# Two transformer layers on one core: output transposes as a stage of their own, modulation chunks in two steps, another order of the streams

## The chip, the cores and the metric

One core of a Trainium2 chip. The metric is the device time of one execution in microseconds, the median of the runs.

## What is computed

The block runs two trunk layers over 512 latent tokens and 256 context tokens of width 1024, in float32. Layer 0 is differential attention with 8 heads, layer 1 is neighbourhood attention with 16 heads of 64. Each is followed by a squared-ReLU MLP of width 4096, and each sub-layer is normed, shifted, scaled and gated by vectors that come from the conditioning (the modulation).

```python
def diff_attend(q, k, v, lam):
    s = jnp.einsum('bqhmd,bkhmd->bhmqk', q, k).astype(jnp.float32) * ATTN_SCALE
    p = jax.nn.softmax(s, axis=-1)
    w = (p[:, :, 0] - lam * p[:, :, 1]).astype(v.dtype)
    return jnp.einsum('bhqk,bkhe->bqhe', w, v)
...
mod_l = jnp.split((jax.nn.silu(c) @ w_mod[i] + b_mod[i])[:, None, :], N_MOD, axis=-1)
h_l = modulate(rms_norm(x, norm1_g[i]), mod_l[0], mod_l[1])
...
x = x + mod_l[2] * y_l
x = x + mod_l[5] * squared_relu_mlp(modulate(rms_norm(x, norm2_g[i]), mod_l[3], mod_l[4]), w_mlp1[i], w_mlp2[i])
```

In layer 0 the output of a head is normed per token (`subln_g`) before the output projection. The context tokens go through the same weights and read only context.

## The kernel before

All matmuls of the model run as three passes over operands that are split into a high and a low part (`PASSES`), so each weight tile is loaded raw (tile `R`, two buffers, queue of SP), copied by ACT (L116) and subtracted by POOL (L117) into a tile `W`. The raw modulation weights use the same two buffers (L130).

**The stages.** Setup with head 0's projections (to about 102 us of the profile), the heads of layer 0 (to 518), its output projection (to 645), its MLP (to 1230), the groups of layer 1, two heads each (to 1550), its output projection (to 1650), its MLP.

**A head of layer 0.** Two generators describe it. `qkv0` projects the 768 tokens in six tiles of 128 (24 matmuls of 384 columns each, in two halves, L370), norms queries and keys (`qk_normed`: ACT L377 and L379, DVE L381, a power on POOL L258, DVE L383), splits the values (L422, L423), rotates on POOL (L427 to L437), and after two tiles turns queries and keys with PE (`turn`, L445, bank `PC`) and splits them (`q_split`, `k_split`, L393 to L407). The fourth step of `k_split`, the copy of the low part into the other half of the partitions, is POOL's (L407). `attend0` works on six query tiles in stages: stage 0 is the scores (L492, one buffer `PS` of three banks, then maximum, exponential and the difference of the two maps on DVE and ACT, L497 to L504), stage 1 the transposes of the map (L516, bank `PB`, split by ACT L518 and DVE L519 into `X`), stage 2 the weighting with the values (L527, bank `PB`) and the norm of the output (ACT L530 and L534, DVE L531 and L252, power on POOL L258, DVE L536, into `O`). The output transpose `turn` (L480, bank `PB`, read out by ACT L481) of a tile is issued at the end of the weighting of the tile after it, and that of the last tile at the very end of the head; then the head's output goes to memory.

**A group of layer 1** has the same shape (`qkv1`, `attend1`): projections in L370, turns of queries and keys in L589 and L591, scores in L632, transposes in L662, weighting in L677 with its read-out in L682 and L683.

**What sets the order.** `run` steps the generators by a string: `q` the projections of the next head, `a` the attention of the present one, `b` the first stage of the next, `p` the rest of an earlier projection, `r` the projection after that, `l` the load of a modulation chunk, `m` its computation. Inside the head and group loops PE keeps the order of this program (`manual_schedule`); ACT, DVE and POOL are ordered by a scheduler at build time. Each engine works its own list strictly in order. `mod_chunk` computes 256 modulation values: 8 matmuls (L222) into a bank `PA`, a copy by ACT (L225), and right behind these on PE either two small matmuls (L235) or one (L227) that read the copy, and a step on DVE.

Of the kernel before, what the change touches and what calls it, by code (L numbers as in the profile page):

```python
# [10 lines left out]
F32 = mybir.dt.float32  # L11
# [7 lines left out]
P = 128  # L19
# [15 lines left out]

ORD_HEAD = "aa qq aa q p q l a q a q m l a qq a q aaa q m aaa qq a q b a q aa"
ORD_OUT0 = "q l aaaa p a m l a m a q a q aaa q aaa qq a q a qq aa Q"
ORD_FIRST1 = "qqqqqqqqqqqq rr q a"
ORD_GROUP = "qq a q a qq a a q a q a aa qqq a a r q a r b"
ORD_GROUP7 = "qq a q a qq a a q a q a aa l qqq a a m q a b"  # L40
ORD_OUT1 = "q a l a m a l aa m a q aa q a q a qq a l m Q"
# [15 lines left out]
class Block:  # L57
# [158 lines left out]
    def mod_chunk(self, l, n, raws):  # L216
# [7 lines left out]
        sb = self.sbt('T', [P, 256])  # L224
        nc.scalar.activation(sb, ps[:, 0:256], AF.Copy)  # L225
        if sec in (2, 5):
            nc.tensor.matmul(ps[0:32, 256:512], self.sel, sb, start=True, stop=True)  # L227
            br = self.sbt('T', [2, 256])
            nc.scalar.dma_start(
                br, self.a["bmod"][l, sec:sec + 1, 256 * qtr:256 * qtr + 256].to_broadcast([2, 256]))  # L230
            nc.vector.tensor_add(br, ps[0:2, 256:512], br)
            nc.scalar.dma_start(self.gates[l, sec // 3, :, 256 * qtr:256 * qtr + 256], br)
            return
        for b in range(2):
# [6 lines left out]
        if sec % 3 == 0:  # L241
            nc.vector.tensor_add(self.mB[:, l, norm, ks, :], src, bias)
        else:
            t = self.sbt('SQ', [P, 2, 2])
            nc.vector.tensor_add(t, src, bias)
            nc.vector.scalar_tensor_tensor(
                self.mA[:, l, norm, ks, :], t, 1.0, self.gT[:, norm, l, ks, None].to_broadcast([P, 2, 2]),
                op0=ALU.add, op1=ALU.mult)


# [148 lines left out]

    def k_split(self, ps, kh, kl, cols):  # L400
        nc = self.nc
        lo, hi = slice(0, 64), slice(64, 128)
        for m, (a, b) in enumerate(((lo, hi), (hi, lo))):
            nc.scalar.activation(kh[a, m, cols], ps[a], AF.Copy)
            nc.vector.tensor_sub(kl[a, m, cols], ps[a], kh[a, m, cols].bitcast(F32))
            nc.scalar.activation(kh[b, m, cols], ps[a], AF.Copy)
            nc.gpsimd.tensor_copy(kl[b, m, cols], kl[a, m, cols].bitcast(F32))  # L407

# [4 lines left out]
    def qkv0(self, w, hT, out, accs=None, tag='Q'):  # L413
# [25 lines left out]
        def turn(i):  # L439
# [7 lines left out]
            self.q_split(ps[:, 0:256], q, cols)  # L447
            self.k_split(ps[:, 256:512], kh, kl, cols)

# [19 lines left out]
    def attend0(self, h, qkv, last=None):  # L469
        nc = self.nc  # L470
        q, kh, kl, v = qkv
        oTs = []
        late = []

        def turn(i, on):
# [4 lines left out]
            nc.tensor.transpose(pt[:, :P], on, self.ident)  # L480
            nc.scalar.activation(oT[:, P * i:P * i + P], pt[:, :P], AF.Copy, scale=self.subg[:, 0:1])  # L481
# [39 lines left out]
        def weigh(i):  # L521
# [4 lines left out]
            for x, kt in jobs:  # L526
# [15 lines left out]
        soft, wTs = {}, {}  # L542
        scores(0)
        yield
        for stage, i in ATT0:
            (scores, turned, weigh)[stage](i)
            yield
        turn(*late.pop(0))
        if last is None:
            nc.scalar.dma_start(self.oT0[h], oTs[0])  # L550
        else:
            last.append(oTs[0])


# [14 lines left out]
    def qkv1(self, w, hT, out, tag='H'):  # L569
# [14 lines left out]
        def turn(i0):  # L584
# [7 lines left out]
            if i0:  # L592
                self.q_split(ps[:, 256:512], q, slice(P * i0 - 256, P * i0), gain=self.gqk)
            self.k_split(ps[:, :256], kh, kl, slice(P * i0, P * i0 + 256))
# [262 lines left out]
class Mods:  # L857


    def __init__(self, b, todo):  # L860
        self.b, self.todo, self.ready = b, todo, []

    def load(self, early=False):
        if self.todo:
            self.ready.append(self.b.mod_load(*self.todo.pop(0), early))

    def chunk(self):
        if self.ready:
            self.b.mod_chunk(*self.ready.pop(0))


def run(mods, order, **streams):


    for s in order.replace(" ", ""):
        if s == "l":
            mods.load()
        elif s == "m":
            mods.chunk()
        elif s.isupper():  # L880
# [6 lines left out]
def hybrid_block(tc, a, out):  # L887
    nc = tc.nc
    with ExitStack() as ctx, ExitStack() as st:
# [19 lines left out]
        with b.psum_phase("psA", **PS_ATTN0):  # L909
            att = b.attend0(0, cur)  # L910
            run(mods, "a", a=att)
            ahead = iter(())
            with tc.manual_schedule(engines={mybir.EngineType.PE}):
                for h in range(1, HEADS0):
# [9 lines left out]
            run(mods, ORD_OUT0, a=att, p=ahead, q=b.project(0, a["woa"], b.oT0, last, 0, lambda i: xs[i], 'H', 'Q', 'S', done))  # L924
            xh, hT2 = done
# [124 lines left out]
```

## Time and profile before

| | us |
|---|---|
| median of 3 runs | 2017.05 (2016.19 to 2019.93) |
| the profiled execution | 2019.41 |
| its span | 2017.6 |
| mean granted TensorE clock | 0.954 |
| PE busy | 1814.1 |
| DVE, ACT, POOL busy | 1156.3, 810.3, 808.7 |

A window row gives a stretch of the span and its length, then the busy time of each engine with the number of its instructions, then the clock granted to PE, the share of DMA and GB/s. A row of waits gives engine, line and tile of the waiting instruction, who ended the wait, the total, the number and the longest. A row of the timeline gives start and length, engine, line, operation, tile written and tiles read, how many instructions are merged, and in brackets how long the engine stood before it and who ended that.

### The profile page before, as it was taken

What the parts mean: (1) busy time and instruction counts of PE and PEld (TensorE: products, weight loads), DVE (VectorE), ACT (ScalarE), POOL (GpSimd) and SP (SyncE); (2) the same over time, 40 slices, a digit from 0 to 9 for tenths busy, and PEclk for the clock granted to TensorE, in tenths of its full rate; (3) what the DMA queues carried; (4) which work ended last, traced back from release to release, by engine and by line L of the source; (5) the groups of instructions that cost most, each with busy time, mean ns of one, the idle gap of its engine ahead of it and who ended that gap; (6) DMA issues with size and microseconds to landing.
All of it is one profiled execution on the core that took longest, in us unless ns stands there. A gap on an engine that the chain in (4) does not pass through costs nothing.

```text
span 2017.6 us, 27149 instructions
## 1 busy us (share of the span) xinstructions
PE 1814.1 (90%) x10256; PEld 1588.0 (79%) x10256; DVE 1156.3 (57%) x2159; ACT 810.3 (40%) x1819; POOL 808.7 (40%) x716
## 2 busy tenths in 40 slices
PE   6497887888789999999999998898888889999998
PEld 5386777788568988888889887888887678888886
DVE  4566666766666434343343586677767574444447
ACT  4355555655634221221222134656656333222331
POOL 3635554544522221222232345444453234443443
PEclk9698888999799999999999998999999889999999
DMA  7212212121612332332422233222233422323232
GB/s 289 68 38 81 66 61 81 53 71 56 212 63 84 104 114 96 126 126 96 129 79 64 63 87 92 53 53 53 60 82 106 136 89 84 104 95 95 86 102 73
DMA packets 59299, 185.03 MB, mean 92 GB/s; under 512 B 7392, under 2 KB 13856, under 8 KB 55584
## 3 DMA queue, kind: packets, MB, share of 16 engines
q1 hardware_dynamic: 53424, 173.44, 28.1%
q10 hardware_dynamic: 5744, 9.85, 1.4%
q8 instruction: 81, 1.33, 0.3%
q14 instruction: 50, 0.41, 0.1%
HBM read 174.45 MB, written 8.81 MB: 91 GB/s over the span
## 4 chain that ended last, share of the span: by engine, by line
PE 67%; DVE 11%; POOL 7%; issue 5%; ACT 5%; DMA 3%; SPq 0%; ACTq 0%; POOLq 0%; DVEq 0%
PE PD L794 21%; PE PA L370 11%; PE PA L829 11%; PE PB L829 9%; PE PA L723 3%; POOL W L117 2%; PE PA L222 2%; POOL SQ L258 1%; PE PS L492 1%; POOL X L566 1%; PE PB L677 1%; PE PB L527 1%; PE PQ L360 1%; ACT E L498 1%; DVE SA L497 1%
## 5 line engine op out<-in xcount | busy, mean ns | idle before, releaser
L117 POOL TENSOR_TENSOR W<-R,W 128x1024 fp32r<-128x1024 f32 (+1 forms) x200 | 449.5, 2255 | 643.5 <-ACT W L116 629.6
L116 ACT ACTIVATE W<-R 128x1024 fp32r<-128x1024 f32 (+1 forms) x204 | 200.5, 993 | 462.2 <-PE PB L829 375.1
L794 PE MATMUL PD<-Q,W 128*128 128x384 f32 (+1 forms) x1584 | 291.6, 334 | 1.2 <-DVE Q L295 0.7
L794 PEld LDWEIGHTS PD<-Q,W 128*128 128x128 f32 x1584 | 271.8, 188 | 13.9 <-issue 5.4
L370 PE MATMUL PA<-W,H 128*128 128x384 f32 x1008 | 204.9, 355 | 0.0
L803 DVE TENSOR_TENSOR N<-N 128x768 f32<-128x768 f32 (+1 forms) x64 | 64.4, 1008 | 223.5 <-ACT N L799 117.1
L794 PE MATMUL PD<-H,W 128*128 128x512 f32 (+1 forms) x816 | 184.2, 382 | 3.4 <-DVE H L296 2.5
L370 PEld LDWEIGHTS PA<-W,H 128*128 128x128 f32 x1008 | 185.1, 199 | 1.0
L258 POOL TENSOR_TENSOR SQ<-SQ,half 128x4 f32<-128x4 f32 (+1 forms) x96 | 97.1, 1012 | 212.2 <-DVE SQ L381 210.5
L370 PE MATMUL PA<-W,Q 128*128 128x384 f32 (+1 forms) x1008 | 177.4, 331 | 1.1 <-POOL W L117 1.1
L794 PEld LDWEIGHTS PD<-H,W 128*128 128x128 f32 x816 | 149.5, 192 | 32.9 <-DVE H L296 2.7
L829 PE MATMUL PA<-W,H 128*128 128x512 f32 x648 | 165.4, 395 | 2.5 <-DVE T L835 2.3
L370 PEld LDWEIGHTS PA<-W,Q 128*128 128x128 f32 x1008 | 163.8, 197 | 1.9 <-POOL W L117 1.9
L829 PEld LDWEIGHTS PA<-W,H 128*128 128x128 f32 x648 | 119.3, 188 | 30.0 <-issue 4.5
L829 PE MATMUL PB<-W,H 128*128 128x512 f32 x504 | 130.3, 391 | 0.0
L829 PE MATMUL PA<-W,Q 128*128 128x512 f32 x432 | 110.4, 395 | 2.2 <-ACT Q L805 1.6
L829 PEld LDWEIGHTS PB<-W,H 128*128 128x128 f32 x504 | 94.3, 188 | 18.5
L498 ACT ACTIVATE E<-PS,SA 128x768 f32<-128x768 f32 (+1 forms) x96 | 72.9, 760 | 72.4 <-DVE SA L497 72.2
L829 PEld LDWEIGHTS PA<-W,Q 128*128 128x128 f32 x432 | 81.2, 188 | 22.1 <-ACT Q L805 2.4
L840 DVE TENSOR_TENSOR H<-PA,H 128x512 f32<-128x512 f32 x78 | 53.7, 688 | 73.2 <-PE PA L829 73.2
L497 DVE TENSOR_REDUCE SA<-PS 128x1 f32<-128x768 f32 (+1 forms) x96 | 74.5, 776 | 32.8 <-ACT E L498 18.5
L492 PE MATMUL PS<-Q,Q 128*128 128x256 f32 (+1 forms) x320 | 71.5, 360 | 22.3 <-ACT E L498 12.0
(215 smaller groups left out, 3131.5 us busy)
## 6 DMA issues: line engine op xcount, KB each, us to landing
R<-in_w_dram SPq DMA_DIRECT2D x128, 512.0 KB
W<-in_wmod_dram SPq DMA_DIRECT2D x28, 1024.0 KB
R<-in_wmod_dram SPq DMA_DIRECT2D x40, 512.0 KB
R<-in_wqa_dram SPq DMA_DIRECT2D x32, 384.0 KB
R<-in_wqb_dram SPq DMA_DIRECT2D x32, 384.0 KB
X<-in_rpb_dram SPq DMA_DIRECT2D x48, 128.0 KB
R<-in_woa_dram SPq DMA_DIRECT2D x8, 512.0 KB
R<-in_wob_dram SPq DMA_DIRECT2D x8, 512.0 KB
```

The source lines that it names most:

```text
L116: nc.scalar.activation(w[:, 0, :n], raw, AF.Copy)
L117: (eng or nc.gpsimd).tensor_sub(w[:, 1, :n], raw, w[:, 0, :n].bitcast(F32))
L258: nc.gpsimd.tensor_tensor(r, ss, self.half[:, :n], op=ALU.pow)
L370: nc.tensor.matmul(acc[:, :n], hT[kt][:, x, P * i:P * i + P], w[kt // 2][:, y, o:o + n], start=(kt == 0 and p == 0), stop=(kt == KT - 1 an ...
L492: nc.tensor.matmul(s[:, c0:c1], q[:, m, P * i:P * i + P], k[:, m, c0:c1], start=p == 0, stop=p == 1)
L497: nc.vector.tensor_reduce(mx, s, op=ALU.max, axis=AX, negate=True)
L498: nc.scalar.activation(e[:, m, :nk], s, AF.Exp, bias=mx[:, 0:1], accum_out=sm[:, m:m + 1])
L723: nc.tensor.matmul(ps, oHL[h][:, x, c:c + P], w[h // 2][:, y, 512 * (h % 2):512 * (h % 2) + 512], start=(first and h == hs[0] and p == 0), ...
L794: nc.tensor.matmul(ps[:, at:at + b1 - b0], w[kt // 4][:, x, o:o + P], hT[kt][:, y, b0:b1], start=(kt == 0 and p == 0), stop=(kt == KT - 1 ...
L803: nc.vector.tensor_mul(r, r, r)
L829: nc.tensor.matmul(ps, hd[:, x, P * i - c0:P * i - c0 + P], w[f][:, y, 512 * n:512 * n + 512], start=(f == 0 and p == 0), stop=(f == len(h ...
L840: nc.vector.tensor_add(av, ps, av)
```

## The change

Six edits belong together.

1. The output transpose of layer 0 is a stage of its own, number 3, in the table `ATT0`, and stands two or more stages behind its weighting. The last weighting and the last two transposes of a head are run by the next head's iteration (stream `z`), ahead of the turn of that head's last queries and keys.
2. `mod_chunk` is a generator of two steps: `m` issues the matmuls and ACT's copy, `n` the small matmuls and the rest. One more chunk is computed in the output stage of layer 0 and one fewer in its MLP.
3. Head 1 has an order of its own (`ORD_HEAD0`), which begins with two tiles of its projections; before, head 0's first scores came first and outside the loop.
4. The streams of the heads and groups are interleaved in another order (one of the lines stands in the diff for all).
5. In layer 1 the turns of queries and keys come one or two half tiles later, and three steps of the next group's projections stand in a group in place of two.
6. In the last turn of queries and keys of a head or group, `k_split` makes the second low part by a DVE subtraction from PSUM in place of POOL's copy.

```diff
-ORD_HEAD = "aa qq aa q p q l a q a q m l a qq a q aaa q m aaa qq a q b a q aa"
+ORD_HEAD0 = "l qqqq a q a q a m aa q n a q aa q a l a q aa m aa q n aaa q a q aa b q a"
+ORD_HEAD = "a q z a q z aa q z p q l a q aa q m l q a q a n q aa m aa q n aa q aa qq aa b q a"
...
-ATT0 = ((0, 1), (1, 0), (2, 0), (1, 1), (2, 1), (0, 2), (0, 3), (1, 2), (2, 2), (0, 4), (1, 3), (2, 3),
-        (0, 5), (1, 4), (2, 4), (1, 5), (2, 5))
+ATT0 = ((0, 1), (1, 0), (2, 0), (1, 1), (2, 1), (0, 2), (3, 0), (0, 3), (1, 2), (3, 1), (2, 2), (0, 4), (1, 3),
+        (3, 2), (2, 3), (0, 5), (1, 4), (3, 3), (2, 4), (1, 5), (2, 5), (3, 4), (3, 5))
@@ mod_chunk
         nc.scalar.activation(sb, ps[:, 0:256], AF.Copy)
+        yield
         if sec in (2, 5):
@@ k_split
-            nc.gpsimd.tensor_copy(kl[b, m, cols], kl[a, m, cols].bitcast(F32))
+            if soon:
+                nc.vector.tensor_sub(kl[b, m, cols], ps[a], kh[a, m, cols].bitcast(F32))
+            else:
+                nc.gpsimd.tensor_copy(kl[b, m, cols], kl[a, m, cols].bitcast(F32))
@@ attend0, weigh
-            late.append((i, on))
-            if len(late) > 1:
-                turn(*late.pop(0))
+            ons[i] = on
@@ qkv1
-                if (i, half) in ((3, 0), (4, 1)):
-                    turn(0 if i == 3 else 2)
+                if (i, half) in ((3, 1), (5, 1)):
+                    turn(i - 3)
                     yield
@@ hybrid_block
-            att = b.attend0(0, cur)
-            run(mods, "a", a=att)
-            ahead = iter(())
+            att, before, ahead = b.attend0(0, cur), iter(()), iter(())
...
-                    run(mods, ORD_HEAD, q=qkv, a=att, b=att2, p=ahead)
-                    att, ahead = att2, qkv
+                    run(mods, ORD_HEAD if h > 1 else ORD_HEAD0, q=qkv, a=att, b=att2, p=ahead, z=before)
+                    before, att, ahead = att, att2, qkv
```

What stands in the lists, at three places. PE ahead of head 0's third scores, before: `PA_723`, `PA_770` and `PA_802` are head 0's turns of queries and keys, `PS_840` its first scores, `W_664` and so on head 1's weights.

```order
L445 MATMUL PA_723<-ident,Y_686 128x128 x2
L445 MATMUL PA_770<-ident,Y_708 128x128 x2
L445 MATMUL PA_723<-ident,Y_697 128x128 x2
L492 MATMUL PS_840<-Q_684,Q_683 128x256
L492 MATMUL PS_840<-Q_685,Q_683 128x256
L492 MATMUL PS_840<-Q_684,Q_683 128x256
L445 MATMUL PA_802<-ident,Y_755 128x128 x2
```

The same place after: `PA_868` is the first tile of head 1's projections; a second whole tile follows these rows, then the scores.

```order
L375 MATMUL PA_868<-W_664,H_318 128x384 x3
L375 MATMUL PA_868<-W_664,H_325 128x384 x3
L375 MATMUL PA_868<-W_669,H_371 128x384 x3
L375 MATMUL PA_868<-W_669,H_378 128x384 x3
L453 MATMUL PA_723<-ident,Y_686 128x128 x2
L375 MATMUL PA_868<-W_674,H_460 128x384 x3
L375 MATMUL PA_868<-W_674,H_467 128x384 x3
L375 MATMUL PA_868<-W_679,H_549 128x384
L453 MATMUL PA_770<-ident,Y_708 128x128 x2
L453 MATMUL PA_723<-ident,Y_697 128x128 x2
```

Projections of head 1 have moved from behind head 0's first scores to ahead of them. Next, PE at the end of a steady head, before: `X_2125` is the map of query tile 5, `O_2085` and `O_2182` are the outputs of tiles 4 and 5, `PS_2217` the next head's second scores.

```order
L370 MATMUL PA_2094<-W_870,H_460 128x384 x3
L370 MATMUL PA_2094<-W_870,H_467 128x384 x3
L370 MATMUL PA_2094<-W_875,H_549 128x384 x3
L370 MATMUL PA_2094<-W_875,H_556 128x384 x3
L527 MATMUL PB_2165<-Q_902,X_2125 128x256 x12
L480 MATMUL PB_2188<-ident,O_2085 128x128
L480 MATMUL PB_2191<-ident,O_2182 128x128
L492 MATMUL PS_2217<-Q_1564,Q_1563 128x256
```

After, the rows from the transposes of tile 5 (`E_2689`) to its weighting (`X_2825`): `PS_2860` is the next head's second scores, `PA_2880` the first tile of the head after next's projections.

```order
L523 MATMUL PB_2826<-ident,E_2689 128x128 x3
L523 MATMUL PB_2832<-ident,E_2689 128x128 x3
L499 MATMUL PS_2860<-Q_2205,Q_2204 128x256
L499 MATMUL PS_2860<-Q_2206,Q_2204 128x256
L499 MATMUL PS_2860<-Q_2205,Q_2204 128x256
L499 MATMUL PS_2860<-Q_2206,Q_2204 128x256
L375 MATMUL PA_2880<-W_2167,H_318 128x384 x3
L375 MATMUL PA_2880<-W_2167,H_325 128x384 x3
L375 MATMUL PA_2880<-W_2172,H_371 128x384 x3
L375 MATMUL PA_2880<-W_2172,H_378 128x384 x3
L534 MATMUL PB_2893<-Q_1526,X_2825 128x256 x12
```

ACT's list at that place after: the read-outs of those transposes stand ahead of the second exponential of the next head's first scores (`PS_2782`).

```order
L411 ACTIVATE Q_2205<-PC_2724 64x256
L409 ACTIVATE Q_2205<-PC_2724 64x256
L525 ACTIVATE X_2825<-PB_2826 128x384
L525 ACTIVATE X_2825<-PB_2832 128x384
L505 ACTIVATE E_2780,SA_2781<-PS_2782,SA_2790 128x256
```

The two output transposes have left the end of the head; the one of tile 5 now comes 13 rows after its weighting, behind the next projections. Last, PE near the end of a group of layer 1, before: `PB_12723` is the third weighting, `E_12630` the map of the fourth unit.

```order
L677 MATMUL PB_12723<-N_12656,H_11722 128x128 x2
L677 MATMUL PB_12723<-N_12656,V_11726 128x128 x2
L662 MATMUL PB_12738<-ident,E_12630 128x128 x4
L662 MATMUL PB_12745<-ident,E_12630 128x128 x4
L370 MATMUL PA_12757<-W_12388,Q_6637 128x256 x3
```

After: `Y_12682` is the last tile's queries and keys, `E_12645` the map of the fourth unit, whose transposes now stand behind a tile of the next group's projections (`PA_12778`) and the last turn of queries and keys.

```order
L375 MATMUL PA_12778<-W_12418,Q_6661 128x256 x3
L375 MATMUL PA_12778<-W_12418,Q_6662 128x256 x3
L595 MATMUL PA_12813<-ident,Y_12593 128x128
L597 MATMUL PA_12813<-ident,Y_12593 128x128
L595 MATMUL PA_12813<-ident,Y_12682 128x128
L597 MATMUL PA_12813<-ident,Y_12682 128x128
L668 MATMUL PB_12836<-ident,E_12645 128x128 x4
L668 MATMUL PB_12843<-ident,E_12645 128x128 x4
```

The transposes of the fourth unit have moved from right behind the third weighting to a tile and a turn after it.

More of the change, by code (lines that the diff above doesn't have):

```diff
@@ L472, in attend0, with turn @@
         oTs = []
-        late = []
-        def turn(i, on):
+        def turn(i):
             if not oTs:
@@ L479, in turn @@
             pt = self.pst('B')
-            nc.tensor.transpose(pt[:, :P], on, self.ident)
+            nc.tensor.transpose(pt[:, :P], ons.pop(i), self.ident)
             nc.scalar.activation(oT[:, P * i:P * i + P], pt[:, :P], AF.Copy, scale=self.subg[:, 0:1])
@@ L545, in attend0 @@
         for stage, i in ATT0:
-            (scores, turned, weigh)[stage](i)
-            yield
-        turn(*late.pop(0))
+            (scores, turned, weigh, turn)[stage](i)
+            if (stage, i) != ATT0[-1]:
+                yield
         if last is None:
@@ L878, in run @@
         elif s == "m":
-            mods.chunk()
+            mods.begin()
+        elif s == "n":
+            mods.end()
         elif s.isupper():
```

37 lines of the change are left out of this document (24 added, 13 removed).

## The prediction

> **What bounds the kernel now.** The page first, then the windows cut at the first queries-and-keys matmul of each head of layer 0 and of a group of layer 1 (columns: stretch, length, then busy time of PE, its weight loads, DVE, ACT and POOL, then the granted clock), then PE's own waits.
>
> ```profile
> PE 1814.1 (90%) x10256; PEld 1588.0 (79%) x10256; DVE 1156.3 (57%) x2159; ACT 810.3 (40%) x1819; POOL 808.7 (40%) x716
> ```
> ```profile
> 102.25:163.65 61.40, 51.02 (x321) 46.70 (x320) 41.55 (x85) 32.95 (x95) 30.65 (x40) 0.89 0.18 55
> 224.91:285.79 60.88, 49.95 (x327) 46.10 (x327) 42.26 (x91) 34.66 (x100) 30.85 (x41) 0.92 0.21 68
> 408.53:463.12 54.59, 49.12 (x327) 45.83 (x327) 37.78 (x93) 31.70 (x96) 23.27 (x36) 0.97 0.16 53
> 463.12:518.00 54.88, 49.02 (x322) 44.65 (x320) 38.79 (x88) 33.27 (x97) 23.02 (x33) 0.97 0.25 81
> 1393.26:1435.44 42.18, 36.57 (x259) 35.63 (x259) 30.88 (x72) 25.69 (x66) 21.00 (x27) 1.00 0.28 63
> ```
> ```profile
> PE PB L480 <- DVE O L536: 47.3, 13, 5.2
> PE PA L589 <- DVE Y L383: 10.9, 5, 2.4
> PE PS L492 <- DVE Q L423: 9.8, 1, 9.8
> PE PA L235 <- ACT T L225: 8.8, 8, 1.3
> PE PB L662 <- DVE T L683: 8.8, 7, 2.5
> PE PS L632 <- POOL H L407: 7.5, 6, 1.9
> ```
>
> PE is the busiest engine in every stretch, but a head of layer 0 leaves it idle for 10.9 us of 60.9, and a group of layer 1 for 5.6 of 42.2. No other engine is near its limit there (DVE 42.3 of 60.9). The largest wait is that of the output transpose (L480) for the normalised output (L536), 47.3 us in 13 times; the change addresses it and each of the others listed. The end of a head, PE first, then DVE and POOL, then the end of a head that has no weights left to split:
>
> ```profile
> 274.02 1.69 PE L527 MATMUL PB<-Q,X 128*128 128x256 f32 x12 [0.42 <-DVE X L519]
> 278.55 0.45 PE L480 MATMUL PB<-ident,O 128*128 128x128 f32 x1 [2.83 <-DVE O L536]
> 284.06 0.45 PE L480 MATMUL PB<-ident,O 128*128 128x128 f32 x1 [5.07 <-DVE O L536]
> 282.04 1.88 DVE L536 SCALAR_TENSOR_TENSOR O<-O,SO,one 128x128 f32<-128x128 f32 x1 [1.12 <-POOL SO L258]
> 281.97 1.80 POOL L117 TENSOR_TENSOR W<-R,W 128x768 fp32r<-128x768 f32 x1
> 457.40 1.60 PE L527 MATMUL PB<-Q,X 128*128 128x256 f32 x12
> 461.98 0.30 PE L480 MATMUL PB<-ident,O 128*128 128x128 f32 x1 [2.87 <-DVE O L536]
> ```
>
> From the last weighting (ends 275.71) to the last turn takes 8.4 us where POOL splits weights, 3.0 without (459.00 to 461.98), and PE stands. DVE's L536 takes 1.88 beside a 1.80 weight split, and 0.35 in the head without one (at 461.48). [...] The change takes no split away; it takes PE away from behind it.
>
> **Head 1, the start.**
>
> ```profile
> 76.63 1.84 POOL L117 TENSOR_TENSOR W<-R,W 128x768 fp32r<-128x768 f32 x1
> 98.16 0.72 POOL L437 TENSOR_TENSOR Y<-Y,Y 128x256 f32<-128x256 f32 x1
> 102.25 6.92 PE L370 MATMUL PA<-W,H 128*128 128x384 f32 x24
> 109.62 4.41 PE L370 MATMUL PA<-W,H 128*128 128x384 f32 x24
> 116.56 1.56 PE L492 MATMUL PS<-Q,Q 128*128 128x512 f32 x8
> ```
>
> PE begins head 1's projections at 102.25, though its fourth weight tile is split by 78.47. The order now puts two tiles of it before head 0's first scores, three and a half before scores(2); before, two and a half. What scores(2) waits for is the last Y: 98.9 now, about 100.3 with one more power and cast ahead on POOL; then eight split steps (99.1 to 104.0 in this trace, so 4.5 more: 105), the first weighting's subtraction behind them on DVE, and some 4 us of PE. So scores(2) starts near 110, not 116.56, with a tile (4.4) and a chunk (1.5) more done: gain 12. Bounds: 6 (head 1's tiles, now evacuated by the same ACT, DVE and POOL, hold up the Y chain by 6 more) and 17 (they don't hold it up, and the 3.4 us behind it close).
>
> **Each head.** At full clock PE's work is 47.4: the 49.1 of the window at 408.53 less what its first matmuls lose to the clock:
>
> ```profile
> 243.85 0.61 PE L235 MATMUL PA<-sel,T 128*128 128x2 f32 x4 [0.92 <-ACT T L225]
> 246.35 2.28 PE L370 MATMUL PA<-W,H 128*128 128x384 f32 x12
> 257.49 1.07 PE L222 MATMUL PA<-R,silu 128*32 128x256 f32 x16
> 259.84 0.61 PE L235 MATMUL PA<-sel,T 128*128 128x2 f32 x4 [1.28 <-ACT T L225]
> 263.92 2.36 PE L370 MATMUL PA<-W,H 128*128 128x384 f32 x12
> 462.78 5.94 PE L370 MATMUL PA<-W,H 128*128 128x384 f32 x24
> ```
>
> After the 2.87 wait 24 matmuls take 5.94, against 4.41: 1.5 lost, and 0.2 in the next lines. After waits of 0.92 and 1.28 twelve keep their 2.3. Gone: both turn waits, their clock loss, and the chunk waits (0.92, 1.28), since the second step stands 3 us or more behind the first. What is late next, by the new order of PE and of ACT:
> - The second tile after a chunk reuses the bank of the tile just ended. Its evacuation took 2.0 (matmuls end 241.93, the last read at 243.97, row below) and the chunk covers 1.07 of it: 0 to 1, I take 0.5.
> - Scores(2) follow the turn of queries and keys by 5.1 us of PE work (two half tiles, a weighting, the turn itself); the last key split stands behind a weighting's normalisation on DVE: 0 to 1.8, I take 0.9. The moved POOL copy adds DVE two operations of 0.43 per head and leaves POOL two of 0.4.
> - The next head's second scores need the first one's exponentials read out, and ACT has these behind the two evacuations of a transpose that PE issues right ahead (first and last row: the points above and below this one):
>
> ```profile
> 243.69 0.28 DVE L423 TENSOR_TENSOR Q<-PA,Q 128x128 fp32r<-128x128 f32 x1
> 254.62 0.82 PE L516 MATMUL PB<-ident,E 128*128 128x128 f32 x6
> 255.63 0.87 ACT L518 ACTIVATE X<-PB 128x384 fp32r<-128x384 f32 x2
> 273.15 0.47 ACT L498 ACTIVATE E<-PS,SA 128x256 f32<-128x256 f32 x1 [0.97 <-DVE SA L497]
> 268.81 1.01 DVE L504 SCALAR_TENSOR_TENSOR E<-E,SA 128x768 f32<-128x768 f32 x1
> ```
>
>   From the transposes' end (255.2) to the second evacuation's is 1.3, with 0.47 behind it about 1.7: 1 to 2.
> - Transposes of tile 5 follow its scores by 7.3 of PE work; the chain took 6.3 (scores end 263.5, L504 269.8), now with two weight copies of 0.85 in ACT's queue and possibly a 1.8 split against DVE: 0 to 2, I take 0.8.
>
> With the 0.4 wait for X that is 4.3 (2 to 7): a head of 51.7. The last turn now stands some 5.4 us of PE work behind its weighting in the next head, and POOL has done its splits by then. Gains: heads 1 to 5, 9.5 each (47.5), heads 6 and 7, 3 each (6). With the start, and 1.8 of weighting and turns pushed into the output stage: 12 + 47.5 + 6 - 1.8 = 63.7. The two-buffer weight queue (SP) keeps its order; in a head of 51.7 each transfer still has 4 us or more to spare, an estimate from its moving two modulation tiles within 5 us of the issue at 242.57.
>
> **Layer 1.**
>
> ```profile
> 1338.45 0.66 PE L662 MATMUL PB<-ident,E 128*128 128x128 f32 x4 [2.46 <-DVE T L683]
> 1338.86 4.61 PE L370 MATMUL PA<-W,Q 128*128 128x256 f32 x24
> 1344.86 3.06 PE L370 MATMUL PA<-W,Q 128*128 128x256 f32 x24
> 1350.61 0.39 PE L632 MATMUL PS<-H,H 128*128 128x256 f32 x1 [1.86 <-POOL H L407]
> 1385.65 0.33 PE L589 MATMUL PA<-ident,Y 128*128 128x128 f32 x1 [2.41 <-DVE Y L383]
> ```
>
> The wait for L683's bank goes (3.5 us of matmuls now lie between), with the clock loss behind it (4.61 against 3.06); the wait for POOL's copy goes, since DVE now makes it and 4 us lie between. The one for L383 stays, near 1.7: that row stands on DVE behind the evacuation of the tile that PE has just finished. A weight tile may be 0.5 late. So 36.6 of work and 2.7 of waits, 39.3 against 42.3: 3 for each of six groups, 18 in all; bounds 8 and 28.
>
> **The rest.** The output stage ends in the same two turns and takes a chunk that the MLP loses (1.07 + 0.61 on both sides): 0, within 6 either way. MLPs and the layer-1 output stage: 0, within 2.
>
> **Sum.** 63.7 + 18 = 82. The profiled execution took 2019.41, so 1937; the median of the runs lies 2.4 lower, which gives 1935.
>
> **Rivals.**
> - *The waits come back inside the head.* ACT and DVE are in-order; if the estimates above go to their upper ends and a split hits the path twice (2 x 1.8), a head takes some 56.5, 4.8 more in seven: 1970. For it: DVE would be busy 43 of 51.7. Against: heads 6 and 7 ran in 54.6 even with their turn waits. Chance 0.15.
> - *Slower: the clock.* Several short waits per head instead of one long one might hold the clock down throughout. Seven heads and seven groups hold 7 x (47.4 + 36.6) = 588 us of full-clock work. At a granted clock of 0.86 it takes 96 more: 2031. It breaks even with before where it costs 82, at 0.88. Against it: waits of 0.92 and 1.28 left the matmuls behind them at full speed, and the group at 1393.26 has a clock of 1.00 with 5.6 of waits. Chance 0.05. [...]
> - *Heads stay at their length* because something else sets it, such as the two raw-weight buffers. Then the start and layer 1 are the gain: 12 + 18, 1987. Against: the weightless heads are 6.5 shorter. Chance 0.05.
>
> **How the numbers follow.** The forecast has 0.73. Its own bounds: heads with 2 to 7 of waits (minus 16, plus 19), and start, layer 1 and rest (10 each way, not all at once): 1909 to 1964; the first rival stretches it to 1972. The second and third, 0.10, and the 0.03 of no change stay out of it. About 0.2% is what a measurement can tell here. Faster 0.92: forecast, first and third rival less 0.01; slower 0.05: the clock; same 0.03: milder cases of it and what I overlook.
>
> **What would show it.** Right: no L480-type wait above 1 us in the heads, head period 50 to 53, head 1's projections from about 71, clock 0.97 or more, groups near 39. Wrong: a scores or transpose line of the heads waiting 3 us or more on ACT or DVE; a head period still near 60.

## The result and the profile after

| | before | after |
|---|---|---|
| median of 4 runs, us | 2018.49 (2016.19 to 2019.98) | 1995.86 (1994.21 to 2000.51) |
| ratio, 95% interval | | 0.9893 [0.9872, 0.9914] |
| profiled execution: span | 2017.6 | 1992.5 |
| mean granted clock | 0.954 | 0.961 |
| layer 0's MLP begins | 636.6 | 612.2 |
| layer 1 and its output stage | 468.1 | 469.0 |

The changed kernel is faster by 1.1%, some 23 us, where 82 were forecast and 1909 us was the lowest and 1972 the highest time of the range. The last two rows are read from the first and last matmul of each MLP in the trace (columns: count, then shortest, median and longest in ns, then the start of the first and of the last). Before, then after:

```profile
L794 PE MATMUL PD<-Q,W x1584: 274/337/444, 636.6 to 1177.0; 128*128 128x384 f32 x180, 128*128 128x256 f32 x18
L794 PE MATMUL PD<-H,W x816: 278/389/583, 1645.1 to 1987.5; 128*128 128x512 f32 x144, 128*128 128x256 f32 x20
```
```profile
L800 PE MATMUL PD<-Q,W x1584: 274/337/444, 612.2 to 1151.0; 128*128 128x384 f32 x180, 128*128 128x256 f32 x18
L800 PE MATMUL PD<-H,W x816: 278/389/583, 1620.0 to 1962.0; 128*128 128x512 f32 x144, 128*128 128x256 f32 x20
```

Layer 0 up to its MLP is 24.4 shorter, layer 1 (1151.0 to 1620.0, before 1177.0 to 1645.1) not at all. All line numbers from here on are those of the changed kernel: scores L499, maximum L504, exponential L505, difference of the maps L511, transposes L523 and their split L525 and L526, weighting L534, output norm L543, output transpose L487, weight copy and split L118 and L119, in layer 1 weighting L683 and split of its transposes L670. The page's line of busy times, then PE's waits, after:

```profile
PE 1826.0 (92%) x10256; PEld 1592.5 (80%) x10256; DVE 1174.4 (59%) x2191; ACT 808.4 (41%) x1819; POOL 793.1 (40%) x684
```

```profile
PE PS L499 <- ACT E L505: 27.4, 14, 4.4
PE PB L683 <- DVE N L670: 16.5, 18, 2.9
...
PE PA L595 <- DVE Y L388: 8.5, 5, 2.8
PE PB L487 <- DVE O L543: 5.6, 4, 4.0
PE PA L375 <- DVE Q L431: 5.0, 7, 4.0
PE PB L534 <- ACT X L525: 4.8, 1, 4.8
```

The wait that the change addressed is gone (47.3 before, 5.6 now, hardly any of it in the heads), and so are the chunks' waits. In their place two others have grown: that of the scores for the exponential (27.4, before 12.0) and that of layer 1's weighting for DVE's split (16.5, before 0.6).

The heads, cut at the second turn of queries and keys of each: one with weights to split, before and after, then the last one, before and after (two kernels, so two pairs of fences):

```profile
266.11:327.27 61.16, 50.23 (x327) 46.39 (x326) 42.28 (x91) 34.66 (x100) 30.87 (x40) 0.92 0.21 68
...
450.08:505.05 54.97, 49.19 (x323) 45.09 (x322) 37.95 (x91) 31.75 (x96) 24.50 (x36) 0.97 0.17 55
```
```profile
254.57:312.45 57.88, 51.17 (x328) 46.72 (x327) 41.09 (x93) 34.72 (x101) 29.26 (x39) 0.94 0.21 71
...
428.37:481.22 52.85, 48.56 (x325) 43.54 (x323) 38.08 (x93) 31.81 (x97) 22.04 (x35) 1.00 0.14 48
```

A head takes 57.9 where 51.7 were forecast. Its end on PE, then on DVE, POOL and ACT (three timelines, put one behind the other):

```profile
262.86 0.93 PE L523 MATMUL PB<-ident,E 128*128 128x128 f32 x6 [0.66 <-DVE E L511]
267.48 1.23 PE L499 MATMUL PS<-Q,Q 128*128 128x256 f32 x4 [3.69 <-ACT E L505]
268.50 4.04 PE L375 MATMUL PA<-W,H 128*128 128x384 f32 x12
```
```profile
260.30 2.51 DVE L511 SCALAR_TENSOR_TENSOR E<-E,SA 128x768 f32<-128x768 f32 x1
...
264.15 0.42 DVE L504 TENSOR_REDUCE SA<-PS 128x1 f32<-128x256 f32 x1 [0.25 <-ACT E L505]
```
```profile
260.14 1.84 POOL L119 TENSOR_TENSOR W<-R,W 128x768 fp32r<-128x768 f32 x1
```
```profile
263.55 0.47 ACT L505 ACTIVATE E<-PS,SA 128x256 f32<-128x256 f32 x1
...
264.02 0.83 ACT L118 ACTIVATE W<-R 128x768 fp32r<-128x768 f32 x1
264.75 0.37 ACT L382 ACTIVATE Y<-PA 128x256 f32<-128x256 f32 x1
265.01 0.28 ACT L430 ACTIVATE Q<-PA 128x128 fp32r<-128x128 f32 x1
265.31 0.38 ACT L411 ACTIVATE Q<-PC 64x256 fp32r<-64x256 f32 x1
265.70 0.38 ACT L409 ACTIVATE Q<-PC 64x256 fp32r<-64x256 f32 x1
266.10 0.87 ACT L525 ACTIVATE X<-PB 128x384 fp32r<-128x384 f32 x2
266.86 0.48 ACT L505 ACTIVATE E<-PS,SA 128x256 f32<-128x256 f32 x1
```

Read from the end: the next head's second scores wait 3.69 for the bank, until the second exponential of its first scores has read it. The maximum for that was ready at 264.57. ACT, in order, had a weight copy, a projection tile's evacuation (L382, L430), two copies of the turn (L411, L409) and both evacuations of the transposes ahead of the exponential, and began it at 266.86. The transposes themselves had ended on PE at 263.79: 2.3 of the wait are the work that ACT did before it came to them. DVE in turn had reached these maxima late, since L511 took 2.51 beside a split on POOL and 1.02 without one. Behind the wait 12 matmuls take 4.04 where 2.25 to 2.33 is usual: the clock granted to PE is 0.50 there (268.50 to 272.54), and 1.00 where 12 take 2.25 (439.30 to 441.55).

Two theories for the heads were told apart. A: the splits on POOL stretch DVE's operations, and everything behind them is late. B: the next head's second scores stand too close behind the first ones on PE, and ACT's order does the rest, splits or not.

### The profile page after: what moved, and what is told of

Its sections match the earlier page's. It is cut to its first block, busy times and chain, and to the rows that moved or that the text cites. A ratio compares the mean times of both kernels' runs of the same rounds, so it can differ in the third digit from the quotient of the medians.

```text
span 1992.5 us, 27095 instructions
## 1 busy us (share of the span) xinstructions
PE 1826.0 (92%) x10256; PEld 1592.5 (80%) x10256; DVE 1174.4 (59%) x2191; ACT 808.4 (41%) x1819; POOL 793.1 (40%) x684
## 4 chain that ended last, share of the span: by engine, by line
PE 68%; DVE 15%; ACT 6%; DMA 4%; issue 4%; POOL 2%; SPq 0%; ACTq 0%; POOLq 0%; DVEq 0%
PE PD L800 21%; PE PA L375 11%; PE PA L835 10%; PE PB L835 9%; PE PA L729 4%; PE PS L499 2%; PE PA L224 2%; PE PB L534 2%; PE PB L683 1%; PE PQ L365 1%; DVE SA L504 1%; ACT E L505 1%; ACT W L118 1%; DVE N L278 1%; DMA R<-in_wqb_dram 1%
## 5 line engine op out<-in xcount | busy, mean ns | idle before, releaser
L119 POOL TENSOR_TENSOR W<-R,W 128x1024 fp32r<-128x1024 f32 (+1 forms) x200 | 452.0, 2268 | 686.3 <-ACT W L118 648.2
L118 ACT ACTIVATE W<-R 128x1024 fp32r<-128x1024 f32 (+1 forms) x204 | 199.7, 995 | 460.3 <-PE PB L835 357.1
L375 PE MATMUL PA<-W,H 128*128 128x384 f32 x1008 | 210.7, 360 | 10.3 <-DVE Q L431 5.0
L375 PE MATMUL PA<-W,Q 128*128 128x384 f32 (+1 forms) x1008 | 172.8, 325 | 2.2 <-ACT H L411 2.2
L375 PEld LDWEIGHTS PA<-W,Q 128*128 128x128 f32 x1008 | 159.1, 192 | 2.4 <-ACT H L411 2.4
L263 POOL TENSOR_TENSOR SQ<-SQ,half 128x4 f32<-128x4 f32 (+1 forms) x96 | 92.7, 968 | 167.9 <-DVE SQ L386 158.8
L499 PE MATMUL PS<-Q,Q 128*128 128x256 f32 (+1 forms) x320 | 72.2, 360 | 30.7 <-ACT E L505 27.4
L835 PEld LDWEIGHTS PA<-W,Q 128*128 128x128 f32 x432 | 81.2, 188 | 22.1 <-ACT Q L811 2.4
L504 DVE TENSOR_REDUCE SA<-PS 128x1 f32<-128x768 f32 (+1 forms) x96 | 74.5, 776 | 27.9 <-PE PS L499 14.4
L505 ACT ACTIVATE E<-PS,SA 128x768 f32<-128x768 f32 (+1 forms) x96 | 72.8, 759 | 39.2 <-DVE SA L504 39.2
```

The source lines that it names most:

```text
L118: nc.scalar.activation(w[:, 0, :n], raw, AF.Copy)
L119: (eng or nc.gpsimd).tensor_sub(w[:, 1, :n], raw, w[:, 0, :n].bitcast(F32))
L263: nc.gpsimd.tensor_tensor(r, ss, self.half[:, :n], op=ALU.pow)
L375: nc.tensor.matmul(acc[:, :n], hT[kt][:, x, P * i:P * i + P], w[kt // 2][:, y, o:o + n], start=(kt == 0 and p == 0), stop=(kt == KT - 1 an ...
L499: nc.tensor.matmul(s[:, c0:c1], q[:, m, P * i:P * i + P], k[:, m, c0:c1], start=p == 0, stop=p == 1)
L504: nc.vector.tensor_reduce(mx, s, op=ALU.max, axis=AX, negate=True)
```

## The experiments

Ratios are to the kernel before; the changed kernel has 0.9893. "MLP 0" is where layer 0's MLP begins, "layer 1" the stretch of the last row of the table above, each from that kernel's trace. A trace is one execution, and the executions of one kernel lie up to 18 us apart (the kernel before: 2014.3 to 2032.0).

| kernel | median us | ratio, 95% interval | MLP 0 | layer 1 |
|---|---|---|---|---|
| before | 2018.5 | | 636.6 | 468.1 |
| after | 1995.9 | 0.9893 [0.9872, 0.9914] | 612.2 | 469.0 |
| 1 heads' weights split by DVE | 1987.1 | 0.9824 [0.9798, 0.9851] | 596.7 | 471.3 |
| 2 second scores later | 1980.1 | 0.9796 [0.9769, 0.9823] | 589.8 | 472.8 |
| 3 layer 1 as before | 1993.6 | 0.9858 [0.9833, 0.9884] | 611.0 | 466.6 |
| 4 chunk in one step | 2010.6 | 0.9948 [0.9929, 0.9968] | 621.4 | 473.1 |
| 5 both 1 and 2 | 1959.0 | 0.9697 [0.9674, 0.9720] | 573.8 | 470.6 |
| 6 layer 1's weighting later | 2011.3 | 0.9948 [0.9928, 0.9969] | 612.1 | 482.5 |
| 7 before, with DVE's splits | 2005.4 | 0.9920 [0.9900, 0.9940] | 623.9 | 468.5 |
| 8 1, 2, 6 and DVE's splits in layer 1 | 1960.8 | 0.9701 [0.9678, 0.9724] | 576.0 | 473.6 |
| 9 5 and DVE's splits in layer 1 | 1957.1 | 0.9688 [0.9662, 0.9714] | 571.9 | 470.5 |
| 10 9 with layer 1's old order | 1949.6 | 0.9647 [0.9621, 0.9674] | 576.8 | 461.6 |
| 11 head 1's old start | 2006.5 | 0.9936 [0.9912, 0.9960] | 619.4 | 474.4 |
| 12 5, moved by half a tile only | 1957.7 | 0.9685 [0.9655, 0.9715] | 571.4 | 475.2 |
| 13 3, copy left on DVE | 1986.3 | 0.9830 [0.9804, 0.9856] | 610.8 | 462.5 |
| 14 10 and 12, copy left on DVE | 1949.2 | 0.9647 [0.9627, 0.9667] | 572.1 | 466.3 |

Layer 1 takes 469.0 to 475.2 in the seven kernels that share its new program (after, 1, 2, 4, 5, 11, 12), so a difference of 3 either way there says nothing.

**1. The splits of the heads' weights on DVE.**

```diff
-                        w = b.load_qkv(a["wqa"], h + 1)
+                        w = b.load_qkv(a["wqa"], h + 1, nc.vector)
```

> The changed kernel, with the low part of head weights in layer 0 subtracted by DVE in place of POOL (four operations of 128x768 per head). It is compared with the changed kernel at 1995.9. Theory A: the splits on POOL stretch DVE operations with two SBUF inputs (L511 took 2.51 beside a split, 1.02 without), and the maximum behind L511, the exponential and the next head's second scores are late by that. Then L511 takes 1.0 at the head's end, the second scores' wait (3.69) falls under 2, the 1.8 of clock loss behind it goes, and a head with splits takes 54 to 55.5 in place of 57.7: about 1980 (1975 to 1986). Theory B: the order of ACT alone sets it (the exponential stands behind two evacuations and a weight copy): the wait stays at 3 or more and the time at 1992 to 1997. If DVE's four added operations (some 0.9 each, by the 1.02 of L511 on 768 columns) land on the path, slower than 1998.

By the ratio it is 14 us faster than the changed kernel, close to what theory A wanted (16), but not where A wanted it. The start first, the third scores of head 0 after and in this kernel; then this kernel's head end on PE, DVE and ACT:

```profile
117.90 1.64 PE L499 MATMUL PS<-Q,Q 128*128 128x512 f32 x8
```
```profile
108.40 1.64 PE L499 MATMUL PS<-Q,Q 128*128 128x512 f32 x8
...
254.53 1.22 PE L499 MATMUL PS<-Q,Q 128*128 128x256 f32 x4 [3.32 <-ACT E L505]
255.55 4.04 PE L375 MATMUL PA<-W,H 128*128 128x384 f32 x12
```
```profile
249.27 1.01 DVE L511 SCALAR_TENSOR_TENSOR E<-E,SA 128x768 f32<-128x768 f32 x1
...
250.59 0.41 DVE L504 TENSOR_REDUCE SA<-PS 128x1 f32<-128x256 f32 x1
```
```profile
253.22 0.49 ACT L525 ACTIVATE X<-PB 128x384 fp32r<-128x384 f32 x1
...
253.91 0.47 ACT L505 ACTIVATE E<-PS,SA 128x256 f32<-128x256 f32 x1
```

At the start 9.5 are gained: there the chain of head 0's tiles ran, in the changed kernel, through DVE operations that took 1.9 to 2.1 beside splits (L388 2.06 at 86.33, beside a split of 1.84; 0.42 at 96.83, without one), and kernel 1 has no such split on POOL. PE also waits less for head 1's weight tiles (twice, 2.14 and 1.63, for POOL's splits in the changed kernel, 0.55 and 0.34 for DVE's here); the two were not told apart. At the head's end L511 takes 1.01 and the maximum is ready at 251.0, yet the exponential begins at 253.91, behind ACT's queue. The wait is 3.32 and the clock loss is the same: 0.94 granted over the head and 4.04 for the 12 matmuls, as in the changed kernel. In the heads theory A is worth about 1 us each (56.9 in place of 57.9), as B has it. One reserve: the scheduler made ACT's list anew, and a second weight copy (0.84, after 0.45 of waiting for its DMA) now stands ahead of the exponential. Kernel 2 has no such change.

**2. The next head's second scores later on PE.** The string of heads 2 to 7:

```diff
-ORD_HEAD = "a q z a q z aa q z p q l a q aa q ...
+ORD_HEAD = "q z a a q z a q z p a q l a q aa q ...
```

> The changed kernel, with the next head's second scores on PE behind one more half tile and the last weighting (2.3 + 1.6 us of work) from head 2 on; only the order string of heads 2 to 7 differs. Theory: the wait of 3.69 and the clock loss of some 1.8 to 2 are there because these scores stand 3.6 us behind the first ones; with 3.9 more in between the wait falls under 1 and a head takes 53 to 55: 1970 to 1982. Rival: the evacuations are late by themselves, and the last weighting (for the split of its transposes) or the first transposes of the second tile wait in its place by as much: 1992 to 2000.

Measured 1980.1, and the head is 53.8 at full clock. Its window, and PE at the same place:

```profile
244.61:298.38 53.77, 48.95 (x328) 44.12 (x327) 40.87 (x93) 34.39 (x101) 28.90 (x39) 1.00 0.23 77
```
```profile
253.58 2.34 PE L375 MATMUL PA<-W,H 128*128 128x384 f32 x12
258.08 1.69 PE L534 MATMUL PB<-Q,X 128*128 128x256 f32 x12 [2.16 <-DVE X L526]
259.61 0.64 PE L499 MATMUL PS<-Q,Q 128*128 128x256 f32 x4
```

The wait of 3.69 for the exponential is gone, the weighting in its place waits 2.16, and behind that the matmuls keep their speed (0.64 for four of the scores, 2.33 for the next 12 of the projections). The chain itself is about as long as before: DVE's split of the transposes (L526) lets the weighting begin 4.25 after their end (258.08 for 253.83); in the changed kernel these splits end 4.63 after it (268.42 for 263.79). Only PE has other work meanwhile. So 4.1 of the forecast's missing 6.2 per head came from the places of stages in the string, and theory B is shown. The string also puts the transposes of the second tile behind one more half tile; no run has one move without the other.

**4. The chunk in one step.**

```diff
         if self.ready:
             self.begun = self.b.mod_chunk(*self.ready.pop(0))
             next(self.begun)
+            next(self.begun)
+            self.begun = None
```

> The changed kernel with the modulation chunk in one step again: its small matmuls stand right behind the large ones on PE. Theory: the waits for ACT's copy of before come back (0.9 to 1.6 for each of some 15 chunks in layer 0's heads and output stage, 16.5 us in all before), and the time is 2006 to 2013. Rival: the time lost there is taken off the waits that PE has later in the head (6.7 per head), so that half or more is hidden: 1996 to 2004.

2010.6; layer 0 up to its MLP is 9.2 longer in the trace, and by the ratio the kernel is 11 longer. The waits are back (9.7 in 7 and 6.7 in 8 times), and over half of them reaches the end: 9 to 11 us, somewhat under half of what the whole change gained, are the chunk's second step.

```profile
PE PA L230 <- ACT T L227: 9.7, 7, 5.0
...
PE PA L239 <- ACT T L227: 6.7, 8, 1.2
```

**11. Head 1's old start.** `ORD_HEAD0` is `"a "` and the string of the other heads without `z` and `p`, so all of head 1 has another order, not its start alone.

> The changed kernel with head 1's order begun as before: head 0's first and second scores ahead of head 1's projections; all else as changed. The forecast gave the start 12: then 2008. Theory now: the third scores came at 117.90 in place of 116.56 with a tile (4.4) and a chunk (1.5) more done, some 4.6 gained: 1998 to 2003. If nothing of that is kept behind it: 1996.

2006.5, nearly what the forecast's 12 would give. From the traces 7.2 stand at the start of the MLP, and in this execution the setup, which the edit leaves as it is, ended 1.8 sooner, so 9. By the ratio it is 9 as well. The third scores' start, 117.90 against 116.56, hid this: what counts is the work done ahead of them. Only 5 of the 9 are there by the end of the heads (the last cut, 484.34 for 481.22, and the 1.8); the other 4 appear in the output stage (135.1 for 131.0), whose PE order a scheduler makes, and why was not tried.

**5, 12. Both edits, and the smaller move.** Kernel 12 moves the scores by the half tile alone and leaves them ahead of the last weighting (`"q a z a q z a ..."`).

> The changed kernel with both edits: head weights of layer 0 split by DVE, and the next head's second scores later on PE. Each alone gave 1987.1 and 1980.1 where the changed kernel gave 1995.9. If the first gains at the start of head 1 (its third tile's scores came 9.5 earlier) and the second in the heads (one took 53.8 in place of 57.8), they add up: about 1971 (1966 to 1975). If the wait of 2.16 for L526 that is left at the head's end belongs to the splits on POOL (DVE's L543 and L388 stand ahead of it there and take 1.4 and 1.8 beside a split), it goes too, 5 heads x 1.5 to 2: 1961 to 1965.

> The kernel with both edits (1959.0), but with the next head's second scores ahead of the last weighting again, so that only half a tile (2.3) is moved before them. Theory: the wait of 3.3 that is left with the splits on DVE becomes about 1, and the wait of the last weighting for L526 (2.16) goes, as the second scores stand ahead of it: within 4 of 1959. Rival: the second exponential stays behind two evacuations in ACT's queue and the scores wait 2 or more per head: 1963 to 1975.

1959.0 and 1957.7. Kernel 5 came out under both ranges of its expectation. In the traces, at the start of the MLP, the two edits gave 15.5 and 22.4 alone and 38.4 together: there they add up. The ranges were made from medians, and the traced executions of 1 and 2 were faster than their medians by 6 and 4. A head of kernel 5:

```profile
235.98:288.28 52.30, 48.43 (x329) 44.18 (x327) 41.46 (x97) 34.57 (x101) 23.51 (x35) 1.00 0.24 79
```

With the clock at 1.00 PE's work is 48.4 and its waits 3.9: close to the head that was forecast (47.4 and 4.3).

**7. The kernel before with DVE's splits.** The edit of 1 in the kernel before.

> The kernel before, with only the head weights of layer 0 split by DVE. Theory: the splits on POOL were what made its two last output transposes wait 8 us in the heads with weights and 3 in those without; then heads 1 to 5 take 56 to 58 in place of 61, the start some 5 less, and the time is about 1995 (1988 to 2002), as much as the whole change gave. Rival: the waits come from the length of the chain behind the last weighting and hardly from the splits: 2010 to 2018.

2005.4, between the two. The start gains (third scores at 107.02, before 116.56), but in the heads the turns keep waiting, 40.5 of 47.3 in all, and heads take 59.5 and 63.4 in turn, the longer ones at a clock of 0.87:

```profile
194.49:257.86 63.37, 53.59 (x327) 49.55 (x326) 41.49 (x95) 34.49 (x100) 24.88 (x36) 0.87 0.20 65
257.86:317.31 59.45, 49.68 (x327) 45.94 (x326) 41.43 (x95) 34.50 (x100) 24.91 (x36) 0.94 0.21 69
```
```profile
PE PB L480 <- DVE O L536: 40.5, 13, 5.5
```
```profile
268.52 0.95 DVE L117 TENSOR_TENSOR W<-R,W 128x768 fp32r<-128x768 f32 x1
...
270.10 0.95 DVE L117 TENSOR_TENSOR W<-R,W 128x768 fp32r<-128x768 f32 x1
...
271.36 0.35 DVE L531 SCALAR_TENSOR_TENSOR O<-PB,SA,O 128x128 f32<-128x128 f32 x1
```

So it is not POOL's splits as such that make the last turn wait. But this kernel does not clear the splits either: two of them now stand on DVE ahead of the norm's first step there, which begins 3.8 after the last weighting's end (271.36 for 267.58). In the head without weights of the kernel before it begins 0.8 after (459.76 for 459.00), and the turn waits 2.87. The turn stands right behind its weighting on PE, and the norm comes late through ACT, DVE and POOL whoever splits; moving the turn took the wait away.

**3, 13. Layer 1 as before, then with the copy left on DVE.**

```diff
-ORD_GROUP = "q a qq a qq aa q a q aa q a q r a r q a r a b"
+ORD_GROUP = "qq a q a qq a a q a q a aa qqq a a r q a r b"
...
-                if (i, half) in ((3, 1), (5, 1)):
-                    turn(i - 3)
+                if (i, half) in ((3, 0), (4, 1)):
+                    turn(0 if i == 3 else 2)
```

Two more order strings go back with these, and kernel 3 also gives the copy of the low part back to POOL.

> The changed kernel with layer 1 as before: its three order strings, the places of its turns, and the copy of the low part on POOL. Theory: layer 1's new order only traded waits (the weighting now waits for DVE's split of the transposes, 16.5 us in 18 times, where before the transposes waited for a bank and the scores for POOL's copy), so the time stays within 4 of 1995.9. Rival, the forecast as made: layer 1 gains 18 and this kernel takes about 2014.

> The changed kernel with layer 1's three order strings and the places of its turns as before, but with the copy of the low part left on DVE: against the run with all of layer 1 as before (1993.6) only that copy differs. The forecast had the wait for POOL's copy (5.6 in that run) among layer 1's gains. If that term is right by itself, 4 to 6 faster than that run: 1987 to 1990. If DVE's two added operations come late in its queue by as much, the same: 1992 to 1996.

1993.6 and 1986.3. The old order is as fast as the new one, or faster by a few us. The copy on DVE gains 4 by the stretch (466.6 to 462.5), in the old order as forecast; the two intervals of the ratios overlap, so it is likely and not shown.

**6. Layer 1's third weighting later.**

```diff
-ORD_GROUP = "q a qq a qq aa q a q aa q a q r a r q a r a b"
+ORD_GROUP = "q a qq a qq aa q a q aa q a q r r a q a r a b"
```

> The changed kernel with the third weighting of a group of layer 1 one projection tile later on PE (order string of groups 1 to 6 only). Theory: layer 1 gained nothing because this weighting follows its transposes by 3.1 us of PE work while ACT and DVE take 6 for them; with 4.4 more of full-clock work (3.1 of matmuls at full clock) in between the wait of 2.9 goes, and in the groups that lose 1.3 of clock behind it that too, 3 to 4 in each of six groups: 1973 to 1980. Rival: the next wait in line (the turn for L388, 1.5 now, or the scores for the key split) takes its place: 1988 to 1998.

2011.3, slower by more than either theory allowed. The weighting's wait falls from 16.5 to 4.9, and the turn behind it, which PE now reaches sooner, waits in its place, 20.1 where it was 8.5, and 3.67 at this spot. PE is slower behind that: the transposes take 1.86 where 1.04 is usual. PE, then POOL:

```profile
1413.18 0.33 PE L595 MATMUL PA<-ident,Y 128*128 128x128 f32 x1 [3.67 <-DVE Y L388]
...
1413.45 1.86 PE L668 MATMUL PB<-ident,E 128*128 128x128 f32 x8
```
```profile
1409.89 1.80 POOL L119 TENSOR_TENSOR W<-R,W 128x768 fp32r<-128x768 f32 x1
1411.65 1.69 POOL L263 TENSOR_TENSOR SQ<-SQ,half 128x4 f32<-128x4 f32 x2
```

The powers that the turn's tiles need (L263) stood behind a weight split and, ahead of that, three additions of another tile (L572, 2.09) on POOL; the norm on DVE began at 1412.70.

**8, 9, 10, 14. DVE's splits in layer 1 too.** Kernel 8 takes the order of 6, 9 that of the change, 10 and 14 the old one.

> The changed kernel with the weights of layer 0's heads and layer 1's groups split by DVE, the next head's second scores later, and the third weighting of a group later. If the parts add up, 1971 for the first two, less some 18 in layer 1: about 1953 (1945 to 1962). If DVE becomes late in layer 1 by the four operations more per group (it is busy 32.5 of 43 there now), layer 1 gives 5 or less: 1964 to 1975.

> The kernel with both edits (1959.0), and the weights of layer 1's groups split by DVE too; the order of layer 1 is that of the changed kernel. Theory: in a group DVE's L649 (0.89 for two, but 2.71 beside a split on POOL) is what makes the third weighting late; without splits on POOL the wait of 2.9 and the 1.3 of clock loss behind it shrink to 1 or less: 6 x 2 to 3 in all, 1941 to 1948. Rival: DVE's four operations more (0.95 each) lie in the same chain and nothing is gained: 1956 to 1964.

> As the run before, but with layer 1's order, turns and copy on POOL as in the kernel before. If the order of layer 1 matters as little without splits on POOL as with them, the same within 4 as the run before. If the waits of the old order (bank of L689, POOL's copy L415) were the splits' work and those of the new order are not, 5 or more faster than it.

> What the runs so far favour, put together: weights split by DVE in the heads and in the groups, the next head's second scores half a tile later, layer 1 in its old order, the copy of the low part on DVE. The parts read from the traces (layer 0 over at 571.4 in the half-tile run, layer 1 and its output stage 461.6 in the run with the old order and DVE's splits, against 576.8 and 461.6 there) give 1944 to 1947. If the copy on DVE is late in a group where DVE has the splits too, 1949 to 1955.

1960.8, 1957.1, 1949.6 and 1949.2. Kernel 8 lies in the range of its first theory, but not for its reason: layer 1 took 473.6, so what 6 lost there came back, and no more. In the new order DVE's splits gain nothing (kernel 9: layer 1 470.5, and 1957.1 for 1959.0), though the longest L649 is 1.48, for 2.04 in the changed kernel. The old order is faster than the new one with DVE's splits: every execution of kernel 10 is faster than every one of kernel 9, by 7.5 in the medians. Whether the old order gains by DVE's splits hangs on the copy: with the copy on POOL layer 1 takes 461.6 (466.6 to 468.5 in the three kernels with POOL's splits: before, 3 and 7), with the copy on DVE 466.3 (kernel 14; 462.5 with POOL's splits, kernel 13). Either seems to gain about 5 alone and both together nothing, in single traces; why was not tried. Kernels 10 and 14 are the fastest here, 3.5% under the kernel before.

## Why the prediction was wrong, point by point

- **Bound and target: right.** PE sets the time. No output transpose in the heads waits over 0.73, and head 1's projections begin at 67.42. A line of the heads' scores does wait over 3 us on ACT, which the prediction had named as what would show it wrong.
- **Where the gap lies.** The spans differ by 25 where 82 were forecast. Of the 57 missing, five heads with splits make 31, layer 1 makes 19 and the start 7; the rest comes out even.
- **Head 1, the start: the order right, the size not.** By the prediction's own mark, the third scores (117.90, not 110) with a tile and a chunk more done, the gain is 4.6; at the first cut of the heads it is 5.4 (138.53 for 143.96). Both lie under the lower bound of 6. Kernel 1, with the splits on DVE, has the third scores at 108.40: head 1's tiles did hold up head 0's, as the case of the lower bound has it, and on top of that DVE's step of the rotation of head 0's tiles (L445) took 1.91 at 90.20, beside a split of 1.86, and 0.42 at 80.1 without one, and the weight tiles came late (2.14 and 1.63). Kernel 11 puts the new order of head 1 at 9 in all, nearer to 12, but 4 of these come from the output stage, of which the forecast said nothing; that is luck.
- **Each head: the step that failed.** It gains 3.3 where 9.5 were forecast for heads with splits. The failed step is "the next head's second scores need the first one's exponentials read out", put at 1.7 with bounds of 1 to 2; the wait was 3.69. The step counted two evacuations and one exponential from the end of the transposes, as if ACT were free by then (the row ends at 255.44, not 255.2, so its sum comes to 1.5). ACT was not: 2.3 of other work stood ahead of the evacuations (263.79 to 266.10), and the evacuations and the exponential then took 1.2, no more than forecast. From this follows the second miss, "clock loss gone": the old loss went, and 2.8 per head are lost behind the new wait (51.17 busy against 48.4 at full clock). The third is the work itself, 48.4 in place of 47.4; why is open. The other waits are near what was forecast: 3.0 in all for 2.6. Sum: 2.4 (waits of 6.7 for 4.3) + 2.8 + 1.0 = 6.2, the gap of 57.9 to 51.7. Kernel 2 gives 4.1 of it back by the places of stages alone, kernel 5 nearly all.
- **The chunk's second step: right.** Kernel 4 loses 9 to 11 without it.
- **Layer 1: failed, 0 for 18.** The step "the wait for L683's bank goes" came true, but the same reordering put the third weighting 3.1 us of projections behind its transposes, whose evacuation takes 6 (1395.4 to 1401.7); that wait (2.92 there, 16.5 in all) was put at nothing, as it was not listed. "The wait for POOL's copy goes" came true (7.5 before; 3.5 are now waited for DVE's subtraction, L413, in its place); that it is worth 4 is likely, not shown (kernel 13). "L589 stays" is right: 8.5 for 10.9. Kernel 6 shows one reason why a gain is hard to have here by order alone: the next chain in line, a tile's norm through POOL, takes over.
- **The rest: right.** Output stage, from the last head's second turn: 130.98, before 131.55.
- **The rivals.** "The waits come back inside the head" is nearest, 56.5 for a head against 57.9, but its cause, a split that hits the path twice, is worth about 1 of it (kernel 1, with the reserve above). "Heads stay at their length" has a time near the measured one, 1987 for 1996, but kernels 2 and 5 shorten the heads with the same two raw-weight buffers, so its cause is not these. "Slower: the clock" did not come: the mean rose from 0.954 to 0.961. In the changed kernel a head's clock is 0.94 with the one wait of 3.69, and 1.00 in kernel 2, which has six waits of 0.2 to 2.16 left.

## What to carry to other kernels

When a wait is removed by moving a stage, work out for every stage that now stands closer to its producer how much PE work lies in between. Compare it with the whole evacuation chain as it queues on ACT and DVE, with all that stands ahead of it there, not with the durations of its own operations. A cheap test of a chain is to move the consumer by one piece of work, as in kernel 2; if the wait just turns up at the next consumer (kernel 6), the chain and not the order has to be shortened. Two edits that help apart need not add up: they did in layer 0 (15.5 and 22.4, together 38.4), and in layer 1 the copy and the splits on DVE did not.

## What was not expected of the hardware

- A DVE operation with one tensor operand and a scalar per partition took longer beside a split on POOL as well: L649 takes 0.48 as a rule and up to 2.04, in the changed kernel:

```profile
L649 DVE TENSOR_SCALAR E<-E,SA x64: 472/483/2035, 1248.6 to 1563.6; 128x512 f32<-128x512 f32 x64
```

  Of its 32 pairs 25 take 0.87 to 0.89. The five that run beside a weight split take 2.43 to 2.83; one of them on DVE, then the split on POOL:

```profile
1398.41 2.71 DVE L649 TENSOR_SCALAR E<-E,SA 128x512 f32<-128x512 f32 x2
```
```profile
1398.16 1.81 POOL L119 TENSOR_TENSOR W<-R,W 128x768 fp32r<-128x768 f32 x1
```

  The other two, 1.42 and 2.12, run beside other operations of POOL (L572 and L722).
- In these traces the length of a wait does not say by itself whether the clock falls behind it. Behind 2.16 (kernel 2) the next 12 matmuls of 384 columns took 2.33, and behind 2.73 they took 2.25, both at a granted clock of 1.00 (that of kernel 2's head, and that of 439.30 to 441.55 in the changed kernel). In the kernel before, 24 matmuls took 4.61 behind 2.46, at a granted clock of 0.63, and 3.06 at 1344.86, at 1.00; 24 of 384 columns took 5.94 behind 2.87, at 0.72, and 4.41 at 109.62, at 1.00. Behind 3.32 (kernel 1) and 3.69 (the changed kernel) 12 took 4.04. The 2.73 is in the changed kernel's last head:

```profile
438.72 0.74 PE L499 MATMUL PS<-Q,Q 128*128 128x256 f32 x4 [2.73 <-ACT E L505]
439.30 2.25 PE L375 MATMUL PA<-W,H 128*128 128x384 f32 x12
```
